# Mixer D's scores from stacked fp32r parts of queries and keys

## The chip, the core and the metric

The kernel runs on one core of a Trainium2 chip. The metric is the device time of one execution in microseconds: 2028.61 us is the median of three runs of the kernel before (2028.13 to 2029.02). A core has TensorE (PE in the profile, its weight loads PEld), VectorE (DVE), ScalarE (ACT), GpSimd (POOL, not used here) and SyncE (SP), which issues most of the DMAs.

## The reference

It is a two-layer encoder trunk: 512 positions, 1024 channels, float32. In each layer one projection feeds four mixers; their outputs are projected, gated, summed and projected again, and a squared-ReLU MLP follows. The change touches mixer D, a dilated sliding-window attention with three groups (window, dilation) of four heads of 64 channels:

```
D_PATTERNS = ((128, 1), (512, 4), (2048, 16))

def mixer_d(q, k, v, cs):                     # q, k, v: 3 groups x 4 heads x 64, rotary on q and k
    for gi, (window, dil) in enumerate(D_PATTERNS):
        # every dil-th position forms a sequence of its own
        o, lse = banded_attention(to_residue(q)..., to_residue(k), to_residue(v), window // (2 * dil), 64)
        ...
    wts = softmax(stack(lses))                # the groups are combined by their softmax denominators
    out = sum(wts[..., None] * stack(outs))

def banded_attention(q, k, v, half_window, block, sink=None):
    sc = einsum(q, k) * hd ** -0.5            # the scores
    sc = where(|kpos - qpos| <= half_window, sc, -1e30)
    p = exp(sc - max(sc)); l = sum(p)
    o = einsum(p, v) / l;  lse = max(sc) + log(l)
```

## The kernel before

**Numbers.** TensorE takes plain fp32 in more than one pass, and fp32r, a float32 with a shorter mantissa, in one. Nearly all large products are written as three fp32r products: every operand is split into a high part (a cast to fp32r) and a low part (what the cast dropped), and high x high, high x low and low x high are summed in PSUM (`mm3`, lines 177 to 179). Weights come as chunks of 128x1024 floats: SP loads a chunk (`raw`, L102), ACT casts it (`whi`, L118), DVE subtracts (`wlo`, L127). `ahead` keeps three chunks loaded and three split before the one in use.

Mixers A and C have their scores in fp32r already, in two products. Their stored queries hold the high part on 64 partitions and the low part on the other 64, stacked, and their keys hold the same high part on both halves, and then the same low part on both; one product of the stack with the doubled high keys and one with the doubled low keys give all four part products (L796, L797).

**Mixer D before.** Queries and keys lie in DRAM (`qD`, `kD`: group, head, 64 channels, 512 positions; in groups 1 and 2 the positions are sorted by residue). `attn_d` loads a group as one tile of queries and one of keys, `Qd` and `Kd`, two heads stacked on the partitions and two side by side, two groups ahead of the first step and the third at the first step of group 1. The heads are walked in 16 steps: in group 0 two steps a head, each with two blocks of 128 queries against 192 or 256 keys; in groups 1 and 2 one step a head, with four blocks of 128 by 128. The scores are plain fp32 products over 64 partitions:

```
nc.tensor.matmul(ps[:, r * 128:(r + 1) * 128], Q[:, r * 128:(r + 1) * 128], K[:, r * 128:(r + 1) * 128])
```

**A step's parts.** Scores (PE into one of two banks `ps_s`); `exps`: DVE adds the mask and takes the maximum (L941, L946 in group 0; L957, L959, L960 in groups 1 and 2), ACT takes the exponentials (L949, L962); `transposes` (PE into `ps_t`, L977, plain fp32); `copies` back to SBUF (L990 on ACT, L988 on DVE where a block has 64 rows); `values` (PE into `ps_o`, plain fp32, L1003 and L1009), with `og` copied out by ACT (L1016, L1018).

**What sets the order.** Every engine runs its instructions in the order in which the code records them. `pipeline` lets steps overlap: in iteration i stand the values of step i-5, the copies of step i-4, the transposes of step i-3, the scores of step i and the exponentials of step i-1:

```
yield from self.pipeline(steps, [("v", 5), ("c", 4), ("t", 3), ("s", 0), ("e", 1)])
```

`merge` lets this generator alternate with `fill`, which records the gate logits and output projection of another branch (here C): fp32r matmuls of 512 columns (L177 to L179), pieces of 6 or more between two iterations, and their results' work on DVE and ACT (L719, L720 gates; L726, L727 gated sums). `MG[2] = (18, 47, 12)` puts twelve of fill's pieces between the first yield of `attn_d`, at which its loads are issued, and its first step. On PE an iteration thus reads: values, transposes, scores, then a row of projection matmuls. Waits between engines are semaphores, set where one touches what another wrote; SP's loads are issued in order too.

Of the kernel before, what the change touches and what calls it, by code (L numbers as in the profile page):

```python
# [11 lines left out]
F32 = mybir.dt.float32  # L12
F32R = mybir.dt.float32r
I32 = mybir.dt.int32
AF = mybir.ActivationFunctionType
ALU = mybir.AluOpType
# [4 lines left out]
DM, S, DEPTH, HD = 1024, 512, 2, 64  # L21
# [54 lines left out]
class Body:  # L76
# [62 lines left out]
    def lows(self):  # L139
        while self.n_lo < self.n_split:  # L140
            self.wlo()
# [622 lines left out]
    def attn_gqa(self, l, which, y):  # L764
# [20 lines left out]
        def step(h, i):  # L785
# [13 lines left out]
            def exps():  # L799
                ps = st["s"]  # L800
                P = st["P"] = ap.tile([128, S], F32, tag="P", name="P", bufs=4)
                m, nm, ls = self.smt(1, "am"), self.smt(1, "an"), self.smt(1, "al")
# [21 lines left out]
            def norm():  # L824
                P, ls = st["P"], st["l"]
                if not isA:
# [62 lines left out]
    def attn_d(self, l, y):  # L889
        nc, ap = self.nc, self.ap  # L890
        nv, ns = nc.vector, nc.scalar
        QK, OG, PO = {}, {}, {}
# [3 lines left out]
        wd = self.drp.tile([12, S], F32, tag="wd", name="wd")  # L896
        steps = []

        def load(g):
            QK[g] = []  # L900
            for src, tag in ((self.qD, "Qd"), (self.kD, "Kd")):
                t = ap.tile([128, 2, S], F32, tag=tag, name=tag, bufs=2)
                nc.sync.dma_start(out=t, in_=src[g].rearrange("(a b) d t -> (b d) a t", b=2))
                QK[g].append(t)

        def window(c):
            return (64, 256) if c == 0 else (0, 192) if c == 3 else (0, 256)
# [1 line left out]
        def step(g, h, u, first, last):  # L909
            hp, o = h // 2, 64 * (h % 2)  # L910
            st = {}

            def scores():
                if first and 0 < g < 2:
                    load(g + 1)
                Q, K = (t[o:o + 64, hp] for t in QK[g])
                ps = st["s"] = self.ps("s")
                if g == 0:
                    for w in range(2):
                        c = 2 * u + w  # L920
                        lo, hi = window(c)
                        k0 = c * 128 - 64
                        nc.tensor.matmul(
                            ps[:, w * 256 + lo:w * 256 + hi], Q[:, c * 128:(c + 1) * 128], K[:, k0 + lo:k0 + hi]
                        )
                else:
                    for r in range(4):
                        nc.tensor.matmul(
                            ps[:, r * 128:(r + 1) * 128], Q[:, r * 128:(r + 1) * 128], K[:, r * 128:(r + 1) * 128]
                        )  # L930

            def exps():
                ps = st["s"]
                P = st["P"] = ap.tile([128, S], F32, tag="P", name="P", bufs=4)
                if g == 0:
                    for w in range(2):
                        c = 2 * u + w
                        lo, hi = window(c)
                        m = self.smt(1, "am")
                        Pw = P[:, w * 256 + lo:w * 256 + hi]  # L940
                        nv.tensor_tensor_reduce(  # L941
                            out=Pw, in0=ps[:, w * 256 + lo:w * 256 + hi], in1=self.cs[:, C_M1 + lo:C_M1 + hi],
                            scale=1.0, scalar=-3.0e38, op0=ALU.add, op1=ALU.max, accum_out=m,
                        )
                        nm = ML[0][:, c, 0, h:h + 1]
                        nv.tensor_scalar(  # L946
                            out=nm, in0=m, scalar1=self.nrs8[:, c:c + 1], scalar2=None, op0=ALU.mult
                        )
                        ns.activation(  # L949
                            out=Pw, in_=Pw, func=AF.Exp, scale=self.rs8[:, c:c + 1], bias=nm,  # L950
                            accum_out=ML[0][:, c, 1, h:h + 1],
                        )
                else:
                    mo = C_M2 if g == 1 else C_M3
                    P3, ps3 = (t.rearrange("p (r k) -> p r k", r=4) for t in (P, ps))
                    mk = self.cs[:, mo:mo + 128].rearrange("p (o k) -> p o k", o=1).to_broadcast([128, 4, 128])
                    nv.tensor_tensor(out=P3, in0=ps3, in1=mk, op=ALU.add)  # L957
                    m = self.smt(4, "dm")
                    nv.tensor_reduce(out=m, in_=P3, axis=AX.X, op=ALU.max, negate=True)  # L959
                    nv.tensor_tensor(out=ML[g][:, :, 0, h], in0=m, in1=self.rs8p, op=ALU.mult)  # L960
                    for r in range(4):
                        ns.activation(  # L962
                            out=P3[:, r], in_=P3[:, r], func=AF.Exp, scale=self.rs8p[:, r:r + 1],
                            bias=ML[g][:, r, 0, h:h + 1], accum_out=ML[g][:, r, 1, h:h + 1],
                        )

            def transposes():
                P = st.pop("P")
                pt = st["t"] = self.ps("t")
                st["n"] = []  # L970
                for b in range(4):
                    lo, n = 0, 128
                    if g == 0 and u == 0 and b == 0:
                        lo, n = 64, 64
                    if g == 0 and u == 1 and b == 3:
                        n = 64
                    nc.tensor.transpose(  # L977
                        pt[0:n, b * 128:(b + 1) * 128], P[:, b * 128 + lo:b * 128 + lo + n], self.ident
                    )
                    st["n"].append(n)  # L980

            def copies():
                pt = st["t"]
                PT = st["T"] = ap.tile([128, S], F32, tag="ptd", name="ptd", bufs=2)
                full = [b for b in range(4) if st["n"][b] == 128]
                for b in range(4):
                    if b not in full:
                        nv.tensor_copy(PT[0:64, b * 128:(b + 1) * 128], pt[0:64, b * 128:(b + 1) * 128])  # L988
                a, z = full[0] * 128, (full[-1] + 1) * 128
                ns.copy(PT[:, a:z], pt[:, a:z])  # L990

            def values():
                PT = st.pop("T")
                if h % 2 == 0 and u == 0:
                    PO[g, hp] = self.ps("o", 1)
                po = PO[g, hp]
                vcol = slice(h * 64, (h + 1) * 64)
                if g == 0:
                    for w in range(2):
                        c = 2 * u + w  # L1000
                        for z in range(2):
                            n = 64 if (c, z) in ((0, 0), (3, 1)) else 128
                            nc.tensor.matmul(  # L1003
                                po[o:o + 64, c * 128:(c + 1) * 128], self.VD[0:n, c + z, vcol],
                                PT[0:n, (2 * w + z) * 128:(2 * w + z + 1) * 128], start=(z == 0), stop=(z == 1),
                            )
                else:
                    for r in range(4):
                        nc.tensor.matmul(  # L1009
                            po[o:o + 64, r * 128:(r + 1) * 128], self.VD[:, (5, 9)[g - 1] + r, vcol],  # L1010
                            PT[:, r * 128:(r + 1) * 128],
                        )
                if h % 2 == 1 and (g > 0 or u == 1):
                    og = ap.tile([128, S], F32, tag=f"og{g}{hp}", name="og", bufs=1)
                    if g == 0:
                        ns.copy(og, po)  # L1016
                    else:
                        ns.copy(  # L1018
                            og.rearrange("p (a r) -> p r a", r=4), po.rearrange("p (r a) -> p r a", r=4)
                        )  # L1020
                    OG[g, hp] = og
                if last:
                    pat = "(c p) n -> p c n" if g == 0 else "(p c) n -> p c n"
                    nc.sync.dma_start(
                        out=mld[g].rearrange(pat, c=4), in_=ML[g].rearrange("p c m h -> p c (m h)")
                    )

            return dict(s=scores, e=exps, t=transposes, c=copies, v=values)

        load(0)  # L1030
        load(1)
        yield
        for g in range(3):
            units = [(h, u) for h in range(4) for u in range(2 if g == 0 else 1)]
            for n, (h, u) in enumerate(units):
                steps.append(step(g, h, u, n == 0, n == len(units) - 1))
# [450 lines left out]
```

## Time and profile before

| what | us |
|---|---|
| median of three runs | 2028.61 |
| the profiled execution | 2031.43 |
| its span (first to last instruction) | 2029.6 |
| PE busy in it | 2007.9 (99%) |
| PEld busy | 1662.9 (82%) |
| DVE busy | 1271.1 (63%) |
| ACT busy | 974.3 (48%) |

PE's busy time counts from a matmul's start to its modelled end, and consecutive matmuls overlap in it; how long one holds up the next is seen from the distance of their starts. A plain fp32 matmul leaves two records (128 records of L928 are 64 matmuls), an fp32r one leaves one, and the types of TensorE's operands read f32 in both cases. Mixer D runs in two places of the span: from 467 to about 563 us in the first layer and from 1470 to about 1566 us in the second.

### The profile page before, as it was taken

The page shows a single profiled execution, that of the slowest core. Times are in us where ns is not written, and L with a number is a line of the kernel's source. Part 1 is how long each engine was busy: PE and PEld are TensorE (multiplying, and loading weights), DVE is VectorE, ACT ScalarE, POOL GpSimd, SP SyncE. Part 2 cuts the span into 40 slices and gives each one's busy share as a digit, 9 for nine tenths or more (in the row PEclk, how much of TensorE's full clock was granted, in tenths as well). Part 3 has the DMA queues.
Part 4 walks back from the last instruction along what each step waited for, and adds up shares of the span by engine and source line. Part 5 has one row for each costly group of instructions (what it writes and reads, how often), then busy time and mean ns, then how long its engine had stood idle before and what let it go on. Part 6 is the DMA issues. An engine that isn't in the chain of part 4 may idle for free.

```text
span 2029.6 us, 25695 instructions
## 1 busy us (share of the span) xinstructions
PE 2007.9 (99%) x9752; PEld 1662.9 (82%) x9752; DVE 1271.1 (63%) x2274; ACT 974.3 (48%) x1701; POOL 0.2 (0%) x4
## 2 busy tenths in 40 slices
PE   9999999999999999999999999999999999999998
PEld 7888789887778888888878888898877888888887
DVE  6879775764466544544658897758644665444445
ACT  4357786854534332322323668868445344322322
POOL 0000000000000000000000000000000000000000
PEclk9999999999999999999999999999999999999999
DMA  5454424332134222323335552152421532323231
GB/s 190 145 156 135 130 66 147 117 125 83 51 106 146 95 95 94 103 94 104 119 109 166 156 166 94 59 163 91 135 73 46 173 96 93 103 94 94 93 104 63
DMA packets 87439, 227.03 MB, mean 112 GB/s; under 512 B 15098, under 2 KB 21370, under 8 KB 87316
## 3 DMA queue, kind: packets, MB, share of 16 engines
q1 hardware_dynamic: 84436, 221.20, 34.3%
q10 hardware_dynamic: 2880, 4.20, 0.6%
q8 instruction: 77, 1.26, 0.3%
q14 instruction: 46, 0.38, 0.1%
HBM read 201.08 MB, written 24.27 MB: 111 GB/s over the span
## 4 chain that ended last, share of the span: by engine, by line
PE 92%; DVE 3%; DMA 2%; ACT 2%; issue 1%; SPq 1%; DVEq 0%; ACTq 0%
PE ps_mm L177 14%; PE ps_mm L178 13%; PE ps_mm L179 13%; PE ps_t L177 6%; PE ps_t L179 6%; PE ps_t L178 6%; PE ps_s L177 6%; PE ps_s L179 6%; PE ps_s L178 6%; PE ps_o L856 2%; PE ps_t L835 2%; PE ps_s L796 1%; PE ps_s L797 1%; PE ps_o L1003 1%; PE ps_t L977 1%
## 5 line engine op out<-in xcount | busy, mean ns | idle before, releaser
L118 ACT CAST whi<-raw 128x1024 fp32r<-128x1024 f32 (+1 forms) x318 | 329.2, 1041 | 333.7 <-PE ps_mm L178 105.9
L127 DVE TENSOR_TENSOR wlo<-raw,whi 128x1024 fp32r<-128x1024 f32 (+1 forms) x318 | 384.8, 1214 | 96.8 <-ACT whi L118 93.9
L177 PE MATMUL ps_mm<-xh,whi 128*128 128x512 f32 x720 | 288.8, 401 | 0.0
L179 PE MATMUL ps_mm<-xh,wlo 128*128 128x512 f32 x720 | 282.4, 392 | 0.0
L178 PE MATMUL ps_mm<-xl,whi 128*128 128x512 f32 x720 | 282.3, 392 | 0.0
L177 PEld LDWEIGHTS ps_mm<-xh,whi 128*128 128x128 f32 x720 | 135.9, 189 | 32.4 <-issue 4.1
L179 PEld LDWEIGHTS ps_mm<-xh,wlo 128*128 128x128 f32 x720 | 135.9, 189 | 29.9
L178 PEld LDWEIGHTS ps_mm<-xl,whi 128*128 128x128 f32 x720 | 136.1, 189 | 26.8
L177 PE MATMUL ps_t<-xh,whi 128*128 128x512 f32 x368 | 143.6, 390 | 0.0
L179 PE MATMUL ps_t<-xh,wlo 128*128 128x512 f32 x368 | 143.3, 389 | 0.0
L178 PE MATMUL ps_t<-xl,whi 128*128 128x512 f32 x368 | 143.2, 389 | 0.0
L177 PE MATMUL ps_s<-xh,whi 128*128 128x512 f32 x352 | 138.5, 393 | 0.0
L179 PE MATMUL ps_s<-xh,wlo 128*128 128x512 f32 x352 | 137.0, 389 | 0.0
L178 PE MATMUL ps_s<-xl,whi 128*128 128x512 f32 x352 | 137.0, 389 | 0.0
L845 DVE TENSOR_TENSOR PT<-ps_t,PT 128x512 fp32r<-128x512 f32 (+2 forms) x128 | 75.1, 587 | 64.3 <-ACT PT L842 56.3
L829 ACT ACTIVATE P<-P,al 128x512 f32<-128x512 f32 (+2 forms) x128 | 82.6, 645 | 17.0 <-DVE al L828 15.7
L719 DVE TENSOR_TENSOR gt<-ps_mm,rb 128x512 f32<-128x512 f32 x54 | 37.2, 689 | 78.9 <-PE ps_mm L179 78.5
L842 ACT CAST PT<-ps_t 128x512 fp32r<-128x512 f32 (+2 forms) x128 | 63.8, 500 | 47.4 <-PE ps_o L856 43.9
L177 PEld LDWEIGHTS ps_t<-xh,whi 128*128 128x128 f32 x368 | 69.1, 188 | 17.2 <-issue 3.0
L179 PEld LDWEIGHTS ps_t<-xh,wlo 128*128 128x128 f32 x368 | 69.1, 188 | 14.9 <-DVE wlo L127 0.5
L178 PEld LDWEIGHTS ps_t<-xl,whi 128*128 128x128 f32 x368 | 69.1, 188 | 14.2
L177 PEld LDWEIGHTS ps_s<-xh,whi 128*128 128x128 f32 x352 | 66.1, 188 | 14.8 <-issue 1.4
(423 smaller groups left out, 4213.5 us busy)
## 6 DMA issues: line engine op xcount, KB each, us to landing
raw<-in_w_dram SPq DMA_DIRECT2D x314, 512.0 KB, 3.5
qsA<-stk SPq DMA_DIRECT2D x32, 128.0 KB, 2.3
qsC<-stk SPq DMA_DIRECT2D x32, 128.0 KB, 2.3
K<-ks SPq DMA_DIRECT2D x16, 256.0 KB, 6.3
Q<-qsA SPq DMA_DIRECT2D x16, 256.0 KB, 3.7
Q<-qsC SPq DMA_DIRECT2D x16, 256.0 KB, 5.1
qD<-stkf SPq DMA_DIRECT2D x24, 128.0 KB, 2.2
kD<-stkf SPq DMA_DIRECT2D x24, 128.0 KB, 2.3
```

The costliest lines, as they stand in the source:

```text
L118: self.nc.scalar.copy(hi[:, s], self.raws[i][:, s])
L127: self.nc.vector.tensor_tensor(out=lo[:, s], in0=raw[:, s], in1=hi[:, s].bitcast(F32), op=ALU.subtract)
L177: mm(ps, sh, mh, start=(k == 0), stop=False)
L178: mm(ps, sh, ml, start=False, stop=False)
L179: mm(ps, sl, mh, start=False, stop=(k == n - 1))
L719: nv.tensor_tensor(out=g, in0=ps, in1=self.rb, op=ALU.mult)
L796: nc.tensor.matmul(ps[:, 0:n], qq, Kt[j][:, 0, b0 * 128:b1 * 128], start=True, stop=False)
L829: ns.activation(out=P[:, 0:n], in_=P[:, 0:n], func=AF.Copy, scale=ls)
L835: nc.tensor.transpose(pt[:, b * 128:(b + 1) * 128], P[:, b * 128:(b + 1) * 128], self.ident)
L842: ns.copy(st["dst"][0], st["src"])
L845: nv.tensor_tensor(out=st["dst"][1], in0=st["src"], in1=st["dst"][0].bitcast(F32), op=ALU.subtract)
L856: nc.tensor.matmul(o, a, b, start=(n_ == 0), stop=(n_ == len(mm) - 1))
```

## The change

Queries and keys of mixer D are loaded by head instead of by group, twice each, onto both halves of the partitions (`Qr`, plain floats, two buffers; the second half of `Kd`, three buffers). `highs(n)` casts both on ACT: all 128 rows of the queries into `Qd`, and the keys into the first half of `Kd`. `lows(n)` subtracts on DVE: rows 64 to 127 of `Qd` become the queries' low part, and the second half of `Kd` the keys' low part. The scores then are two fp32r products of each block, over 128 partitions, as in mixers A and C. The load of head n+2 stands behind the scores of head n, its casts ahead of that head's exponentials, its subtractions behind that head's mask; the first two heads are loaded where the groups were, and cast and subtracted just ahead of the first step. Masks, exponentials, transposes, copies and values are as before.

```
+        def load(n):
+            g, h = heads[n]
+            q = ap.tile([128, S], F32, tag="Qr", name="Qr", bufs=2)
+            k = ap.tile([128, 2, S], F32R, tag="Kd", name="Kd", bufs=3)
+            for z in range(2):
+                nc.sync.dma_start(out=q[64 * z:64 * (z + 1)], in_=self.qD[g, h])
+                nc.sync.dma_start(out=k[64 * z:64 * (z + 1), 1].bitcast(F32), in_=self.kD[g, h])
+        def highs(n):
+            qs = ap.tile([128, S], F32R, tag="Qd", name="Qd", bufs=2)
+            ns.copy(qs, q)
+            ns.copy(k[:, 0], k[:, 1].bitcast(F32))
+        def lows(n):
+            nv.tensor_tensor(out=qs[64:128], in0=q[64:128], in1=qs[64:128].bitcast(F32), op=ALU.subtract)
+            nv.tensor_tensor(out=k[:, 1], in0=k[:, 1].bitcast(F32), in1=k[:, 0].bitcast(F32), op=ALU.subtract)
...
             def scores():
-                Q, K = (t[o:o + 64, hp] for t in QK[g])
+                n = 4 * g + h
+                Q, K = QK[n]
...
+                for o, q0, k0, w in blocks:
+                    for z in range(2):
                         nc.tensor.matmul(
-                            ps[:, w * 256 + lo:w * 256 + hi], Q[:, c * 128:(c + 1) * 128], K[:, k0 + lo:k0 + hi]
+                            ps[:, o:o + w], Q[:, q0:q0 + 128], K[:, z, k0:k0 + w], start=(z == 0), stop=(z == 1)
                         )
+                if g > 0 or u == 1:
+                    QK.pop(n)
+                    if n + 2 < len(heads):
+                        load(n + 2)
...
             def exps():
+                n = 4 * g + h + 2
+                ahead = (g > 0 or u == 1) and n < len(heads)
+                if ahead:
+                    highs(n)
...
+                if ahead:
+                    lows(n)
...
         load(0)
         load(1)
         yield
+        for n in range(2):
+            highs(n)
+            lows(n)
```

On PE, at the first step of group 1 in the first layer, before (L1003 are values, L977 transposes, L928 scores, L177 the next projection matmul; xN counts equal neighbours):

```order
L1003 MATMUL ps_o<-ptd,VD 64x128 x4
L977 MATMUL ps_t<-cs,P 128x128 x3
L977 MATMUL ps_t<-cs,P 64x128
L928 MATMUL ps_s<-Kd,Qd 128x128 x4
L177 MATMUL ps_mm<-xh,whi 128x512
```

And with the change (the same lines have the numbers 1031, 1005 and 946 now):

```order
L1031 MATMUL ps_o<-ptd,VD 64x128 x4
L1005 MATMUL ps_t<-cs,P 128x128 x3
L1005 MATMUL ps_t<-cs,P 64x128
L946 MATMUL ps_s<-Kd,Qd 128x128 x8
L177 MATMUL ps_mm<-xh,whi 128x512
```

The scores stay between the transposes and the projection matmuls; four plain matmuls have become eight fp32r ones.

On DVE, ahead of the first mask of the first layer, before (L726 and L727 are the gated sums of two chunks, L941 the mask, L946 the scaled maximum):

```order
L127 TENSOR_TENSOR wlo<-raw,whi 128x1024
L726 SCALAR_TENSOR_TENSOR gt<-gt,ps_mm 128x512
L727 TENSOR_TENSOR mg<-mg,gt 128x512
L726 SCALAR_TENSOR_TENSOR gt<-gt,ps_mm 128x512
L727 TENSOR_TENSOR mg<-mg,gt 128x512
L941 ISA P,am<-ps_s,cs 128x192
```

With the change (L921 and L922 are `lows`, L967 is the mask):

```order
L127 TENSOR_TENSOR wlo<-raw,whi 128x1024
L726 SCALAR_TENSOR_TENSOR gt<-gt,ps_mm 128x512
L727 TENSOR_TENSOR mg<-mg,gt 128x512
L921 TENSOR_TENSOR Qd<-Qr,Qd 64x512
L922 TENSOR_TENSOR Kd<-Kd 128x512
L921 TENSOR_TENSOR Qd<-Qr,Qd 64x512
L922 TENSOR_TENSOR Kd<-Kd 128x512
L726 SCALAR_TENSOR_TENSOR gt<-gt,ps_mm 128x512
L727 TENSOR_TENSOR mg<-mg,gt 128x512
L967 ISA P,am<-ps_s,cs 128x192
```

The subtractions of the first two heads stand between the gated sums of two chunks, ahead of the first mask, and the first scores wait for the first pair of them.

On ACT, at the first steps of group 1 in the first layer, before (L990 copies transposes, L962 are exponentials, L118 and L720 work for the projections):

```order
L118 CAST whi<-raw 128x1024
L720 ACTIVATE gt<-gt,d_hb 128x512
L990 COPY ptd<-ps_t 128x384
L962 ACTIVATE P,ML_4733<-P,ML_4733,rs8p 128x128 x4
L990 COPY ptd<-ps_t 128x384
L962 ACTIVATE P,ML_4733<-P,ML_4733,rs8p 128x128 x4
```

With the change (L915 and L916 are `highs`, L1018 the copies, L988 the exponentials):

```order
L118 CAST whi<-raw 128x1024
L720 ACTIVATE gt<-gt,d_hb 128x512
L1018 COPY ptd<-ps_t 128x384
L915 CAST Qd<-Qr 128x512
L916 CAST Kd<-Kd 128x512
L988 ACTIVATE P,ML_4733<-P,ML_4733,rs8p 128x128 x4
L1018 COPY ptd<-ps_t 128x384
L915 CAST Qd<-Qr 128x512
L916 CAST Kd<-Kd 128x512
L988 ACTIVATE P,ML_4733<-P,ML_4733,rs8p 128x128 x4
```

Two casts have come ahead of the exponentials of each step that prepares a later head. On SP the loads change in the same way: before, four loads of 512 KB stand ahead of the first step and two at the start of group 1; now eight of 128 KB stand ahead, and four more for each later head, one or two heads between two weight loads.

## Rows read from the trace of the kernel before

**Rows 1.** The page: span, engines' busy time, the chain's shares by engine

```profile
span 2029.6 us, 25695 instructions
...
PE 2007.9 (99%) x9752; PEld 1662.9 (82%) x9752; DVE 1271.1 (63%) x2274; ACT 974.3 (48%) x1701; POOL 0.2 (0%) x4
...
PE 92%; DVE 3%; DMA 2%; ACT 2%; issue 1%; SPq 1%; DVEq 0%; ACTq 0%
```

**Rows 2.** Stretches, layer 1: length; PE, PEld, DVE, ACT, POOL busy; clock; DMA

```profile
467.20:505.00 37.80, 37.80 (x180) 27.23 (x179) 19.78 (x65) 16.11 (x40) 0.00 (x0) 1.00 0.22 76
505.00:551.00 46.00, 46.00 (x260) 35.45 (x259) 21.94 (x38) 26.91 (x79) 0.00 (x0) 1.00 0.16 45
```

**Rows 3.** PE's timeline at the first scores: start, length, engine, line, operation, tiles, form

```profile
460.14 0.39 PE L179 MATMUL ps_mm<-xh,wlo 128*128 128x512 f32 x1
...
466.94 0.39 PE L179 MATMUL ps_mm<-yC,wlo 128*128 128x512 f32 x1
467.25 1.02 PE L923 MATMUL ps_s<-Kd,Qd 64*128 64x192 f32 x4
468.21 0.50 PE L177 MATMUL ps_mm<-xh,whi 128*128 128x512 f32 x1
468.54 0.40 PE L178 MATMUL ps_mm<-xl,whi 128*128 128x512 f32 x1
```

**Rows 4.** PE's timeline: transposes, scores, projection; groups 0 and 2

```profile
498.73 0.63 PE L977 MATMUL ps_t<-cs,P 128*64 128x128 f32 x4
499.29 1.02 PE L923 MATMUL ps_s<-Kd,Qd 64*128 64x256 f32 x4
...
500.58 0.40 PE L178 MATMUL ps_mm<-xl,whi 128*128 128x512 f32 x1
...
544.41 0.66 PE L977 MATMUL ps_t<-cs,P 128*128 128x128 f32 x4
544.99 1.16 PE L928 MATMUL ps_s<-Kd,Qd 64*128 64x128 f32 x8
...
546.42 0.40 PE L178 MATMUL ps_mm<-xl,whi 128*128 128x512 f32 x1
```

**Rows 5.** PE's timeline: transposes and projection without scores between

```profile
550.04 0.66 PE L977 MATMUL ps_t<-cs,P 128*128 128x128 f32 x4
...
550.77 0.39 PE L178 MATMUL ps_mm<-xl,whi 128*128 128x512 f32 x1
```

**Rows 6.** Weight loads of scores: a block's; all of L928, shortest, median, longest

```profile
510.70 0.96 PEld L928 LDWEIGHTS ps_s<-Kd,Qd 64*128 64x128 f32 x8 [0.17 <-issue]
...
L928 PEld LDWEIGHTS ps_s<-Kd,Qd x128: 182/188/188, 505.0 to 1548.9; 64*128 64x128 f32 x128
```

**Rows 7.** PE's timeline in mixer C: fp32r scores, transposes, fp32r matmuls

```profile
362.59 0.28 PE L796 MATMUL ps_s<-K,Q 128*128 128x256 f32 x1
362.71 0.28 PE L797 MATMUL ps_s<-K,Q 128*128 128x256 f32 x1
362.82 0.49 PE L835 MATMUL ps_t<-cs,P 128*128 128x128 f32 x3
363.07 0.36 PE L177 MATMUL ps_mm<-whi,xh 128*128 128x256 f32 x1
363.27 0.28 PE L178 MATMUL ps_mm<-wlo,xh 128*128 128x256 f32 x1
```

**Rows 8.** ACT and DVE ahead of the first scores; casts and subtractions of 128x512

```profile
462.70 0.72 ACT L720 ACTIVATE gt<-gt,d_hb 128x512 f32<-128x512 f32 x1
...
465.37 0.69 DVE L727 TENSOR_TENSOR mg<-mg,gt 128x512 f32<-128x512 f32 x1
...
L870 ACT CAST yC<-yt 128x512 fp32r<-128x512 f32 x8 | 5.0, 621 | 0.7 <-DVE yt L868 0.4
...
L874 DVE TENSOR_TENSOR yC<-yt,yC 128x512 fp32r<-128x512 f32 x8 | 5.5, 686 | 1.4 <-ACT yC L870 1.4
```

**Rows 9.** DMA issues: tiles, queue, count, KB each, median us to landing

```profile
qD<-stkf SPq DMA_DIRECT2D x24, 128.0 KB, 2.2
...
Kd<-kD SPq DMA_DIRECT2D x6, 512.0 KB, 6.0
```

More of the change, by code (lines that the diff above doesn't have):

```diff
@@ L897, in attn_d @@
         steps = []
[L899 to L904, printed above, removed]
+        heads = [(g, h) for g in range(3) for h in range(4)]
+        def load(n):
[5 more added lines that the diff above has]
+                nc.sync.dma_start(out=k[64 * z:64 * (z + 1), 1].bitcast(F32), in_=self.kD[g, h])
+            QK[n] = [q, k]
+        def highs(n):
+            q, k = QK[n]
+            qs = ap.tile([128, S], F32R, tag="Qd", name="Qd", bufs=2)
+            ns.copy(qs, q)
+            ns.copy(k[:, 0], k[:, 1].bitcast(F32))
+            QK[n] = [qs, k, q]
+        def lows(n):
+            qs, k, q = QK[n]
+            nv.tensor_tensor(out=qs[64:128], in0=q[64:128], in1=qs[64:128].bitcast(F32), op=ALU.subtract)
+            nv.tensor_tensor(out=k[:, 1], in0=k[:, 1].bitcast(F32), in1=k[:, 0].bitcast(F32), op=ALU.subtract)
+            QK[n] = [qs, k]
         def window(c):
@@ L913, in scores @@
             def scores():
-                if first and 0 < g < 2:
-                    load(g + 1)
-                Q, K = (t[o:o + 64, hp] for t in QK[g])
+                n = 4 * g + h
+                Q, K = QK[n]
                 ps = st["s"] = self.ps("s")
                 if g == 0:
+                    blocks = []
                     for w in range(2):
@@ L921, in scores @@
                         lo, hi = window(c)
-                        k0 = c * 128 - 64
+                        blocks.append((w * 256 + lo, c * 128, c * 128 - 64 + lo, hi - lo))
+                else:
+                    blocks = [(r * 128, r * 128, r * 128, 128) for r in range(4)]
+                for o, q0, k0, w in blocks:
+                    for z in range(2):
                         nc.tensor.matmul(
-                            ps[:, w * 256 + lo:w * 256 + hi], Q[:, c * 128:(c + 1) * 128], K[:, k0 + lo:k0 + hi]
+                            ps[:, o:o + w], Q[:, q0:q0 + 128], K[:, z, k0:k0 + w], start=(z == 0), stop=(z == 1)
                         )
[L926 to L930, printed above, removed]
+                if g > 0 or u == 1:
+                    QK.pop(n)
+                    if n + 2 < len(heads):
+                        load(n + 2)
             def exps():
```

## The prediction

> **What bounds the kernel now.** I read the page first: its totals and its chain of waits. TensorE is busy 99% of the 2029.6 us and the chain that ended last runs through it for 92% [rows 1]. So a change is worth what it takes from, or adds to, the row of matmuls on PE, unless it starves that row. Second came the busy times of the only stretch that the change touches, mixer D in the first layer: in its 83.8 us PE has no free time at the full granted clock of 1.00, while DVE is busy 41.7 us and ACT 43.0 [rows 2]. The second layer repeats it a thousand microseconds later. Third came PE's timeline there. A busy PE is not a PE at its peak, so I read starts, not durations: from L179 at 460.14 to L179 at 466.94 there are 30 fp32r matmuls of 512 columns, (466.94 - 460.14) / 30 = 0.227 us each, back to back [rows 3]. Whatever lies between two such groups costs the distance of the starts around it, less the matmuls that belong to the groups.
>
> **What one block of scores costs today.** Each layer has 16 steps: eight in group 0 (two blocks of 192 and 256 columns each) and eight in groups 1 and 2 (four blocks of 128). A plain fp32 matmul leaves two records, so a step leaves 4 or 8.
> Group 0 straight after projection matmuls: from L179 at 466.94 to the second L178 behind it at 468.54 is 1.60 us. Two pitches of 0.227 in it belong to the groups: 1.60 - 0.45 = 1.15 us [rows 3]. This is so for the first three steps of a layer, where no transposes stand ahead yet.
> Group 0 behind transposes: from the first L977 at 498.73 to L178 at 500.58 is 1.85 us [rows 4]. Where a step has no scores any more, the same distance is 550.77 - 550.04 = 0.73 us [rows 5]. The block costs 1.12 us (five steps a layer).
> Groups 1 and 2: 546.42 - 544.41 - 0.73 = 1.28 us (eight steps a layer) [rows 4, 5].
> A part of that is no arithmetic. The weight loads of one such block are eight within 0.96 us of 0.188 each, so (0.96 - 0.188) / 7 = 0.110 us apart, and the matmuls follow at about 0.112: eight of them are 0.90 us [rows 6]. The other 0.38 us lie at the two edges of the block, where the next weights are not loaded ahead.
>
> **What it costs after.** The stacked parts need two fp32r matmuls for each block, over 128 rows. The count of records stays the same, 4 and 8; what changes is the price of one and the edges.
> Edges: mixer C has just this sequence already, fp32r scores (L796, L797), then transposes, then fp32r matmuls of 256 columns. L796 to L797 is 0.12 us, L797 to the first of three transposes 0.11, and from that transpose to the second fp32r matmul behind 363.27 - 362.82 = 0.45, which is three transposes of 0.11 and one matmul of 0.12 [rows 7]. No edge is left on either side, and I take none for the new blocks.
> Price: 256 columns at 0.12 us [rows 7]. For 192 and 128 columns in fp32r the trace has no row. From below: the line through 0.12 at 256 columns and 0.227 at 512 gives 0.093 and 0.066. From above: four passes as plain fp32, two records of 0.112 at 128 columns, so 0.224, and 0.336 at 192. I take 0.112 for both: a weight load of 128 columns stands ahead of each, the same number of columns as in the loads that are 0.110 apart now, and that row is the nearest [rows 6].
> Group 0 becomes 2 x 0.112 + 2 x 0.12 = 0.46 us, groups 1 and 2 become 8 x 0.112 = 0.90 us.
> Saved over both layers: 6 x (1.15 - 0.46) + 10 x (1.12 - 0.46) + 16 x (1.28 - 0.90) = 4.1 + 6.6 + 6.1 = 16.8 us. All of it lies on PE's row.
>
> **The added work.** Each of 24 heads gets two casts on ACT, each 128x512 to fp32r, 0.62 us by the nearest row, and two subtractions on DVE, 0.69 each (the 64-row one taken as dear) [rows 8]. Heads 2 to 11 of each layer do this a step or more early. ACT's cover: in the 46 us of groups 1 and 2 it is busy 26.9; six pairs of casts add 7.4, in a stretch that shrinks to 42.9 us, so 34.3 of 42.9, 80%. DVE there goes from 21.9 to 30.2. In the 37.8 us of group 0 it goes from 19.8 to about 28 of 32.9, ACT from 16.1 to 21.1 [rows 2]. Neither reaches its limit. A cast delays the exponentials behind it, but the order has the transposes that read them two steps later, over 4 us each, and weights are split three chunks ahead. I take nothing for these; without the cover, each head could cost up to 1.24 us.
> The first head has no such cover. Its casts stand behind L720, which ends at 462.70 + 0.72 = 463.42, and are done by 464.7. Its subtractions stand on DVE behind L727, which ends at 465.37 + 0.69 = 466.06, and end at 466.06 + 2 x 0.69 = 467.44 [rows 8]. PE is ready at 466.94 + 0.227 = 467.17 [rows 3]. With about 0.1 for the hand-over PE waits 0.4 us, once a layer: +0.8 us. Head 1's subtractions then hold up the gated products (L726) and the first mask by some 1.4 us, which the two score banks and the same two steps cover.
> SP issues four loads of 128 KB a head instead of two of 512 KB a group. A store of 128 KB lands in 2.2 us, the present loads of 512 KB in up to 6.0 [rows 9]. In the order they are free to go once the scores of the head before are done and the weight load ahead of them on SP has gone, at least a step ahead of their cast. I take nothing.
> Sum: -16.8 + 0.8 = -16.0 us. The profiled execution took 2031.43 us, 2.8 above the median, so it would be 2015.4, and the median 2028.61 - 16.0 = 2012.6.
>
> **Rivals.**
> *Narrow fp32r matmuls pay plain fp32's price* (0.224 and 0.336 us). Then group 0 costs 0.67 + 0.24 = 0.91 and groups 1 and 2 1.79: the first saves 6 x 0.24 + 10 x 0.21 = 3.5, the second loses 16 x 0.51 = 8.2, and with the 0.8 it is +5.5: 2034.1, slower. For it: no fp32r row here is under 256 columns. Against it: the rows at 256 and 512 lie near one line, and nothing in them bends up. There are 128 matmuls of 128 columns and 32 of 192; the change turns into a loss once their mean price passes 0.112 + 16.0 / 160 = 0.21 us.
> *The price falls under the weight load's spacing*, to 0.066 and 0.093: 128 x 0.046 + 32 x 0.019 = 6.5 more: 2006.1. Against it: no loads of 128 columns there come closer than about 0.11. The Trainium skill (TensorE: Matmul & The Clock Gate, "Back-to-back issue gap") puts a stream of load and matmul pairs of 128 columns at about 81 ns each; by that, as an estimate, 160 x 0.031 = 5.0 us more would be saved, 2007.6. The loads 0.110 apart speak against it, but they are plain fp32 and so don't settle it.
> *The edges stay*: 32 x 0.38 = 12.2 us of the saving is not there: 2024.8. For it: the step keeps plain fp32 products and transposes ahead of the scores. Against it: mixer C's rows.
> *The split heads come late.* ACT and DVE take their work in order, so a cast that waits for its load holds up exponentials, and a subtraction that waits for its cast holds up the split of a weight. With half a microsecond of it reaching PE for each of the 20 covered heads, that is +10: 2022.6. For it: SP puts loads behind weight loads that wait for DVE, so the three queues close a ring. Against it: the idle shares above. The same skill page ("Architectural detail: the array is 16x 32x32, not 1x 128x128") calls ACT's and DVE's queues strictly first in, first out; the rows fit that and show no price.
>
> **Chances.** Forecast 0.69 (its own range 2010 to 2016, for the wait and a pitch from 0.107 to 0.12), late heads 0.11, edges 0.07, fp32's price 0.07, cheaper than the load 0.06. From 2007 to 2024 lie the first two and about half of the last, the others outside. What can be told from no change is 0.2%, 4.1 us. Faster by more than that: 0.69 + 0.06 + 0.09 of the late heads + 0.02 of the edges = 0.86; within: the rest of the edges, 0.02 of late heads and 0.01 of fp32's price, 0.08; slower 0.06.
>
> **What would show it.** Right: a score record of 128 columns every 0.11 us and of 256 every 0.12, the first L178 after a block of groups 1 and 2 at 0.73 + 0.90 us from the first transpose, a stretch of mixer D about 8 us shorter in each layer, one PE wait of some 0.4 us ahead of a layer's first scores, for DVE. Wrong: a spacing near 0.22, edges of 0.2 us left, or PE waiting inside the stretch for Qd, Kd, wlo or the copies of ACT.

## The result, and the profile after

The changed kernel takes 2013.55 us in the median of four runs (2011.35 to 2016.16) against 2028.37 of the kernel before on the same chip (2027.1 to 2029.02): a ratio of 0.9927, 95% interval 0.9915 to 0.9939, 14.8 us less. Forecast were 2012.6 us and 16.0 less. The profiled execution took 2011.35 us.

The page after answers to [rows 1]; the columns are an engine's busy time, its share and its instructions, then the chain's shares:

```profile
span 2009.6 us, 26003 instructions
...
PE 1988.3 (99%) x9752; PEld 1657.4 (82%) x9752; DVE 1300.8 (65%) x2322; ACT 998.2 (50%) x1749; POOL 0.2 (0%) x4
...
PE 93%; DVE 3%; ACT 2%; DMA 1%; issue 1%; SPq 0%; DVEq 0%; ACTq 0%
```

PE still bounds the kernel. Its count of records is the same, 9752, and its busy time fell by 19.6 us; DVE gained 29.7 us of work and ACT 23.9, which the chain does not show.

Next the whole span cut at mixer D, with the columns of [rows 2]. Of before:

```profile
0.00:467.20 467.20, 460.76 (x2372) 388.95 (x2372) 350.00 (x730) 293.09 (x532) 0.20 (x4) 1.00 0.42 134
467.20:562.50 95.30, 95.30 (x506) 71.69 (x506) 46.55 (x111) 49.74 (x133) 0.00 (x0) 1.00 0.20 62
562.50:1470.30 907.80, 902.53 (x4318) 754.04 (x4317) 581.37 (x996) 432.78 (x709) 0.00 (x0) 1.00 0.37 117
1470.30:1565.60 95.30, 95.30 (x506) 71.67 (x506) 46.55 (x111) 49.75 (x133) 0.00 (x0) 1.00 0.20 62
```

And the same stretches of after:

```profile
0.00:464.10 464.10, 458.66 (x2372) 387.83 (x2373) 350.79 (x732) 295.60 (x535) 0.20 (x4) 1.00 0.42 132
464.10:551.00 86.90, 86.76 (x506) 69.44 (x506) 60.63 (x134) 59.50 (x153) 0.00 (x0) 1.00 0.42 117
551.00:1459.50 908.50, 902.77 (x4318) 754.32 (x4318) 582.11 (x998) 434.60 (x712) 0.00 (x0) 1.00 0.37 116
1459.50:1546.40 86.90, 86.76 (x506) 69.44 (x505) 60.74 (x134) 59.54 (x153) 0.00 (x0) 1.00 0.43 117
```

The two stretches of mixer D went from 95.3 to 86.9 us, 16.8 together. The rest of this pair of profiles differs by 3.1 us ahead of the first mixer D and by less than a microsecond in each part behind it, where nothing was changed. A part of the 3.1 is one stretch in which before shows 0.50 of the granted clock (1.2 GHz in place of 2.4) after PE waited 2.2 us for a load of mixer A's queries, and after does not. Before, then after:

```profile
210.67:214.08 3.41, 3.41 (x10) 2.63 (x9) 3.38 (x9) 3.39 (x7) 0.00 (x0) 0.50 1.04 275
```

```profile
210.67:214.08 3.41, 3.41 (x16) 2.83 (x16) 3.38 (x6) 3.38 (x4) 0.00 (x0) 1.00 0.67 225
```

So the profiled pair differs by 20.1 us and the medians by 14.8; the length of the stage is the better measure. I take it from PE's starts, from the record ahead of a layer's first score to the first record behind its last values (505 steps from record to record): 95.29 us before and 86.84 to 86.86 after, 8.44 to 8.45 less a layer. A second set of runs of the changed kernel gave 86.85 and 86.86, although its profiled execution took 2018.01 us in all. Below, "the stage" is this length.

Now PE's timeline of after at the places of [rows 3] and [rows 4]: the first scores, a block of group 0 and one of group 2 behind transposes (the latter with the values ahead of them):

```profile
463.93 0.39 PE L179 MATMUL ps_mm<-yC,wlo 128*128 128x512 f32 x1
464.16 1.00 PE L946 MATMUL ps_s<-Kd,Qd 128*128 128x192 f32 x4
465.00 0.40 PE L177 MATMUL ps_mm<-xh,whi 128*128 128x512 f32 x1
465.23 0.39 PE L178 MATMUL ps_mm<-xl,whi 128*128 128x512 f32 x1
...
491.22 0.63 PE L1005 MATMUL ps_t<-cs,P 128*64 128x128 f32 x4
491.60 0.68 PE L946 MATMUL ps_s<-Kd,Qd 128*128 128x256 f32 x4
492.12 0.41 PE L177 MATMUL ps_mm<-xh,whi 128*128 128x512 f32 x1
492.38 0.39 PE L178 MATMUL ps_mm<-xl,whi 128*128 128x512 f32 x1
...
532.28 1.09 PE L1037 MATMUL ps_o<-ptd,VD 128*64 128x128 f32 x8
533.30 0.66 PE L1005 MATMUL ps_t<-cs,P 128*128 128x128 f32 x4
533.71 1.09 PE L946 MATMUL ps_s<-Kd,Qd 128*128 128x128 f32 x8
534.64 0.45 PE L177 MATMUL ps_mm<-xh,whi 128*128 128x512 f32 x1
534.93 0.40 PE L178 MATMUL ps_mm<-xl,whi 128*128 128x512 f32 x1
```

By the prediction's own measure the block of group 2 now costs 534.93 - 533.30 - 0.73 = 0.90 us (0.90 forecast), that of group 0 behind transposes 492.38 - 491.22 - 0.73 = 0.43 (0.46). The rows and columns of the array that a matmul uses, called its tile below, stand behind the operands' names: `64*128` for the scores in [rows 3, 4], `128*128` here. Keep an eye on them.

The first block of a layer takes 465.23 - 463.93 - 0.45 = 0.85; the next one, 917 ns between the same two records, costs 0.46. So 0.39 us are a wait, and the groups of PE's weight loads by releaser name it (busy, mean ns | idle before, its releaser):

```profile
L946 PEld LDWEIGHTS ps_s<-Kd,Qd 128*128 128x128 f32 x192 | 24.5, 191 | 1.2 <-DVE Kd L922 0.9
```

DVE's timeline there, as forecast, has the subtractions behind L727:

```profile
462.36 0.69 DVE L727 TENSOR_TENSOR mg<-mg,gt 128x512 f32<-128x512 f32 x1
463.08 0.69 DVE L921 TENSOR_TENSOR Qd<-Qr,Qd 64x512 fp32r<-64x512 f32 x1
463.80 0.69 DVE L922 TENSOR_TENSOR Kd<-Kd 128x512 fp32r<-128x512 f32 x1
```

The keys' low part is done at 464.49. PE was ready at 463.93 + 0.23 = 464.16 and started the block's first product then; the second, which reads the low part, followed 0.39 us later. No other block of scores waits: the 0.9 us are two times, one a layer. The loads that feed the heads take longer than the store of 128 KB that I had read (count, KB each, median us from issue to landing; [rows 9]), with no wait of PE from it:

```profile
Qr<-qD SPq DMA_DIRECT2D x48, 128.0 KB, 3.9
Kd<-kD SPq DMA_DIRECT2D x48, 128.0 KB, 4.0
```

ACT did wait for them: six of the 24 casts of queries stood 9.9 us in all for their load. The longest of these waits:

```profile
477.87 0.62 ACT L915 CAST Qd<-Qr 128x512 fp32r<-128x512 f32 x1 [2.84 <-DMA Qr<-qD]
```

### The profile page after: what moved, and what is told of

It is laid out like the page before. It is cut to its first block, busy times and chain, and to the rows that moved or that the text cites. A ratio compares the mean times of both kernels' runs of the same rounds, so it can differ in the third digit from the quotient of the medians.

```text
span 2009.6 us, 26003 instructions
## 1 busy us (share of the span) xinstructions
PE 1988.3 (99%) x9752; PEld 1657.4 (82%) x9752; DVE 1300.8 (65%) x2322; ACT 998.2 (50%) x1749; POOL 0.2 (0%) x4
## 4 chain that ended last, share of the span: by engine, by line
PE 93%; DVE 3%; ACT 2%; DMA 1%; issue 1%; SPq 0%; DVEq 0%; ACTq 0%
PE ps_mm L177 14%; PE ps_mm L178 14%; PE ps_mm L179 14%; PE ps_t L177 6%; PE ps_t L179 6%; PE ps_t L178 6%; PE ps_s L177 6%; PE ps_s L178 6%; PE ps_s L179 6%; PE ps_o L856 2%; PE ps_t L835 2%; PE ps_s L796 1%; PE ps_s L797 1%; PE ps_s L946 1%; PE ps_o L1031 1%; PE ps_t L1005 1%
## 5 line engine op out<-in xcount | busy, mean ns | idle before, releaser
L118 ACT CAST whi<-raw 128x1024 fp32r<-128x1024 f32 (+1 forms) x318 | 329.1, 1041 | 302.6 <-PE ps_mm L178 94.1
L177 PE MATMUL ps_mm<-xh,whi 128*128 128x512 f32 x720 | 286.3, 398 | 0.0
L179 PE MATMUL ps_mm<-xh,wlo 128*128 128x512 f32 x720 | 281.7, 391 | 0.0
L179 PEld LDWEIGHTS ps_mm<-xh,wlo 128*128 128x128 f32 x720 | 135.6, 188 | 29.7
L177 PEld LDWEIGHTS ps_mm<-xh,whi 128*128 128x128 f32 x720 | 135.7, 188 | 27.3 <-issue 0.8
L177 PE MATMUL ps_t<-xh,whi 128*128 128x512 f32 x368 | 143.6, 390 | 0.0
L179 PE MATMUL ps_t<-xh,wlo 128*128 128x512 f32 x368 | 143.3, 389 | 0.3 <-DVE wlo L127 0.3
L177 PE MATMUL ps_s<-xh,whi 128*128 128x512 f32 x352 | 138.5, 394 | 0.0
L179 PE MATMUL ps_s<-xh,wlo 128*128 128x512 f32 x352 | 137.0, 389 | 0.0
L829 ACT ACTIVATE P<-P,al 128x512 f32<-128x512 f32 (+2 forms) x128 | 82.6, 645 | 16.9 <-DVE al L828 15.7
L177 PEld LDWEIGHTS ps_t<-xh,whi 128*128 128x128 f32 x368 | 69.1, 188 | 17.2 <-issue 3.0
L179 PEld LDWEIGHTS ps_t<-xh,wlo 128*128 128x128 f32 x368 | 69.1, 188 | 15.1 <-DVE wlo L127 0.7
L177 PEld LDWEIGHTS ps_s<-xh,whi 128*128 128x128 f32 x352 | 66.1, 188 | 14.8 <-issue 1.4
L178 PEld LDWEIGHTS ps_s<-xl,whi 128*128 128x128 f32 x352 | 66.1, 188 | 14.0 <-issue 0.5
```

What stands on the lines that cost most here:

```text
L118: self.nc.scalar.copy(hi[:, s], self.raws[i][:, s])
L177: mm(ps, sh, mh, start=(k == 0), stop=False)
L178: mm(ps, sh, ml, start=False, stop=False)
L179: mm(ps, sl, mh, start=False, stop=(k == n - 1))
L829: ns.activation(out=P[:, 0:n], in_=P[:, 0:n], func=AF.Copy, scale=ls)
```

## The experiments

My theory: a block of scores lost its two edges, 0.38 us, because fp32r matmuls have none where plain fp32 has them, and kept the price of 0.112 us a record; the added work is covered. Rivals: that part of the saving comes from elsewhere in the change (other loads, other order), and that the edges belong to something else than the number format.

**Groups 1 and 2 alone.** Group 0 keeps plain fp32 scores over 64 rows, and its heads are loaded but neither cast nor subtracted. The edit of the scores:

```
+                    if g == 0:
+                        nc.tensor.matmul(ps[:, o:o + w], Q[0:64, q0:q0 + 128], K[0:64, 1, k0:k0 + w].bitcast(F32))
+                        continue
```

> Heads of group 0 are loaded as with the change but neither cast nor subtracted, and their scores are plain fp32 matmuls over 64 rows again; groups 1 and 2 are as changed. Theory (each block of scores is worth its own difference on PE's row): the blocks of groups 1 and 2 cost 0.90 us and the 16 of group 0 1.12 to 1.15 again, so 16 x 0.38 = 6.1 us under the kernel before, about 2022.3; no wait ahead of the first scores. Rival (a good part of the gain lies outside the score blocks, in a shorter chain at the end of mixer D or ahead of it): the time lies well under that, near 2016, or near the kernel before.

Measured: 2024.1 us, ratio 0.9976 (0.9965 to 0.9987). The stage is 92.08 us, 3.21 less than before in each layer: eight blocks at 0.38 are 3.1. Group 0 is back at the distances of before (1606, 1490 ns), groups 1 and 2 stand at 1240. The time is 1.8 above the expected one, within what whole runs vary; the stage says that groups 1 and 2 bring about what the sum gave them.

**The feeding alone.** All loads, casts and subtractions, but the scores as before, from the plain copies, which have three buffers here:

```
+            kx = ap.tile([128, 2, S], F32R, tag="Kd", name="Kd", bufs=1)
+            ns.copy(kx[:, 0], k)
...
+            nv.tensor_tensor(out=kx[:, 1], in0=k, in1=kx[:, 0].bitcast(F32), op=ALU.subtract)
...
+                    nc.tensor.matmul(ps[:, o:o + w], Q[0:64, q0:q0 + 128], K[0:64, k0:k0 + w])
```

> All of the added work (four loads a head, two casts, two subtractions at the same places) is there, but its results go unused: the scores are plain fp32 matmuls from the loaded tiles. Theory (the added work is covered): the time of the kernel before, 2028.4, within 1 us; ACT is some 30 us and DVE some 32 us busier over both layers, and PE does not wait for them. Rival (late heads): half a microsecond or more for each of 20 heads reaches PE, 2038 or more.

Measured: 2028.79 us, ratio 0.9998 (0.9989 to 1.0008). The stage is 95.29 us in both layers, as before. The added work costs nothing where PE doesn't wait for its result, and the rival of the late heads falls.

**Half the moving columns.** In groups 1 and 2 the second product has 64 keys in place of 128:

```
+                        v = w // 2 if g > 0 and z == 1 else w
...
-                            ps[:, o:o + w], Q[:, q0:q0 + 128], K[:, z, k0:k0 + w], start=(z == 0), stop=(z == 1)
+                            ps[:, o:o + v], Q[:, q0:q0 + 128], K[:, z, k0:k0 + v], start=(z == 0), stop=(z == 1)
```

> In groups 1 and 2 the second product of each block (with the keys' low part) takes only the first 64 of its 128 columns; the low part of the other keys is left out. Theory (the weight load of 128 columns sets the spacing of narrow fp32r matmuls): the starts in a block stay about 0.11 us apart and the block stays at 0.90 us. Rival (the moving columns set it): the four short ones take about half, and the block falls to about 0.70 us, 3 us in all.

Measured: 2012.24 us in one run, the stage 86.97. PE's timeline:

```profile
534.32 0.66 PE L1006 MATMUL ps_t<-cs,P 128*128 128x128 f32 x4
534.73 1.06 PE L947 MATMUL ps_s<-Kd,Qd 128*128 128x128 f32 x8
535.62 0.47 PE L177 MATMUL ps_mm<-xh,whi 128*128 128x512 f32 x1
535.93 0.40 PE L178 MATMUL ps_mm<-xl,whi 128*128 128x512 f32 x1
```

535.93 - 534.32 = 1.61 against 1.63: at 128 and 64 columns the moving operand is not what sets the price of an fp32r record.

**Half the stationary columns.** The second product of groups 1 and 2 takes only 64 of the 128 queries, and the sums of both products are left out:

```
+                        m = 64 if g > 0 and z == 1 else 128
...
-                            ps[:, o:o + w], Q[:, q0:q0 + 128], K[:, z, k0:k0 + w], start=(z == 0), stop=(z == 1)
+                            ps[0:m, o:o + w], Q[:, q0:q0 + m], K[:, z, k0:k0 + w], start=(g > 0 or z == 0), stop=(g > 0 or z == 1)
```

> As the changed kernel, but in groups 1 and 2 the second of the two products of a block has only 64 queries as its stationary operand and overwrites half of the rows (the sums are left out). Halving the moving columns left the spacing at 0.11 us. Theory that the load of the stationary columns sets it: records after a 64-column load stand some 0.055 us closer, four to a block, so a block's stretch goes from 1.24 to about 1.02 us, and 16 of them give 3.5 us: 2010 us. Rival, that each matmul has a fixed price whatever its operands: 1.24 us and 2013.5 us. Second rival, that the change between 64 and 128 columns costs what the change of rows costs, some 0.1 us at each turn: 1.6 us and 2019 us.

Measured: 2010.38 us in one run, the stage 85.33 to 85.35, 1.5 less a layer.

```profile
535.02 0.66 PE L1006 MATMUL ps_t<-cs,P 128*128 128x128 f32 x4
535.44 0.88 PE L947 MATMUL ps_s<-Kd,Qd 128*128 128x128 f32 x8
536.15 0.44 PE L177 MATMUL ps_mm<-xh,whi 128*128 128x512 f32 x1
536.43 0.39 PE L178 MATMUL ps_mm<-xl,whi 128*128 128x512 f32 x1
```

536.43 - 535.02 = 1.41 in place of 1.63; the spacings of records alternate between about 62 and 112 ns where all were 109 to 115. So the price of 0.11 us of an fp32r record goes with its 128 stationary columns. The Trainium skill (TensorE: Matmul & The Clock Gate, "LDWEIGHTS (loading the stationary operand)") says that a weight load takes time by its columns and not by its rows, by its formula 107 ns for 128 and 53 for 64; the spacings of 0.11 and 0.06 agree. The expectation's second rival fell too. In this run half of the records use 64 columns of the array, in turn with those that use 128:

```profile
L947 PE MATMUL ps_s<-Kd,Qd 128*64 128x128 f32 x64 | 11.8, 224 | 0.0
```

None of these turns shows an edge.

**The stacked operands as plain fp32.** The same tiles over 128 rows, read as plain fp32:

```
-                            ps[:, o:o + w], Q[:, q0:q0 + 128], K[:, z, k0:k0 + w], start=(z == 0), stop=(z == 1)
+                            ps[:, o:o + w], Q[:, q0:q0 + 128].bitcast(F32), K[:, z, k0:k0 + w].bitcast(F32), start=(z == 0), stop=(z == 1)
```

> The same stacked tiles over 128 rows, but the score products are plain fp32 matmuls, two records each. Theory (the edges of 0.2 us belong to plain fp32 matmuls): they are there on both sides of a block; groups 1 and 2 cost 16 x 0.112 + 0.38 = 2.17 us a block, group 0 4 x 0.162 + 4 x 0.216 + 0.38 = 1.89, so 43 us over the changed kernel, about 2056. Rival (the edges came from operands of 64 rows): no edges, 1.79 and 1.51 us, about 2044.

Measured: 2043.39 us in one run, the stage 102.3.

```profile
533.25 0.65 PE L1005 MATMUL ps_t<-cs,P 128*128 128x128 f32 x4
533.75 1.95 PE L946 MATMUL ps_s<-Kd,Qd 128*128 128x128 f32 x16
535.45 0.48 PE L177 MATMUL ps_mm<-yC,whi 128*128 128x512 f32 x1
535.77 0.39 PE L178 MATMUL ps_mm<-yC,whi 128*128 128x512 f32 x1
```

The block costs 535.77 - 533.25 - 0.73 = 1.79 us for 16 records, 0.112 each: plain fp32, and no edge. My theory's cause falls here. What is different from before is the tile, `128*128` in place of `64*128`.

**fp32r over 64 rows.** The changed kernel, with the products cut to the first 64 rows, so that the products with the queries' low part are left out:

```
-                            ps[:, o:o + w], Q[:, q0:q0 + 128], K[:, z, k0:k0 + w], start=(z == 0), stop=(z == 1)
+                            ps[:, o:o + w], Q[0:64, q0:q0 + 128], K[0:64, z, k0:k0 + w], start=(z == 0), stop=(z == 1)
```

> As the changed kernel, but the scores' matmuls of mixer D read only the first 64 rows of the stacked tiles (the products with the queries' low parts are left out); same count, same 128x128x... blocks, fp32r. From the end of the matmul records before a block to the second projection matmul behind it the changed kernel shows 1238 to 1246 ns in groups 1 and 2 and 802 to 810 ns in group 0 behind transposes, without a gap at either edge. Theory that a gap comes with a change between operands of 64 and of 128 rows: about 1.4 to 1.65 us and 1.0 to 1.2 us, with 0.15 to 0.2 us at one edge or both, and some 2019 us in all. Rival, that the gap needs a plain fp32 matmul of 64 rows: 1.24 and 0.81 us as now, and 2013.5 us.

Measured: 2022.56 us in one run, the stage 92.59.

```profile
534.68 0.66 PE L1005 MATMUL ps_t<-cs,P 128*128 128x128 f32 x4
535.27 1.11 PE L946 MATMUL ps_s<-Kd,Qd 64*128 64x128 f32 x8
536.30 0.50 PE L177 MATMUL ps_mm<-xh,whi 128*128 128x512 f32 x1
536.64 0.40 PE L178 MATMUL ps_mm<-xl,whi 128*128 128x512 f32 x1
```

536.64 - 534.68 - 0.73 = 1.23: the edges are back with fp32r. Record by record, against the changed kernel: from the last transpose to the first score 203 ns in place of 29, from the last score to L177 200 in place of 110, and 68 more in the pitches next to these. With the run before, all four cases are there: plain and fp32r, over 64 rows with edges, over 128 without. The cause is the change between 64 and 128 rows from the scores to their neighbours. What happens at an edge shows in PE's weight loads, here and in the changed kernel:

```profile
535.27 0.96 PEld L946 LDWEIGHTS ps_s<-Kd,Qd 64*128 64x128 f32 x8 [0.17 <-issue]
```

```profile
533.69 0.97 PEld L946 LDWEIGHTS ps_s<-Kd,Qd 128*128 128x128 f32 x8
```

Over 64 rows the block's first load starts together with its matmul, 0.17 us after the loads of the transposes; over 128 rows it follows them at once. The Trainium skill (TensorEngine Tiling (Array Packing), "Key Properties") says that a change of the tiling mode drains TensorE; these rows fit that for the rows of the array and give a price, 0.33 us in fp32r and 0.38 in plain fp32 for going to 64 rows and back.

**Values in pairs.** The values (plain fp32 products of 64 stationary columns, tile `128*64`) pay such edges too: 318 ns from L179 to their first record in place of 227, and 203 to the next transposes in place of 109. What brings these edges is not shown: the 64 columns alone don't, since the half-weight scores above have none, and neither have the transposes, which go from `128*128` to `128*64` in 109 ns. So the products of two steps were recorded together:

```
+                second = (u if g == 0 else h) % 2
+                held.append((g, h, u, PT))
+                if not second:
+                    return
+                for a in held:
+                    product(*a)
+                held.clear()
+                close()
```

(`product` and `close` are the two halves of `values` as it was. `ptd` has three buffers in place of two and `P` three in place of four, and a later tile that used `P`'s buffers takes one of `ptd`'s.) The changed kernel ran beside it:

> The changed kernel again, on the chip of the two that follow: 2013.5 us, 0.993 of the kernel before. Blocks of scores as before: 1.24 us in groups 1 and 2, 0.80 to 0.94 us in group 0, the first of a layer 1.30 us.

> The changed kernel with the products by the values of two steps emitted together, so that 16 of the 32 calls of values in the program have no other matmuls around them. Theory: each call pays some 0.14 us at its front edge and 0.15 us behind it, as the trace shows for values between projections and transposes; 16 calls fewer on an edge give 16 x 0.29 = 4.6 us, so 2009 us. Rival: the time at those edges is the wait of TensorE for the copies of the transposes and stays, or the later release of two tiles delays the next step as much as it saves: 2013.5 us or up to 2 us above it.

Measured: the changed kernel 2013.59 us, ratio 0.9929 (0.9915 to 0.9942); paired 2006.38, ratio 0.9892 (0.9876 to 0.9909). The stage went from 86.85 to 84.03, 5.6 us in both layers. The edges explain less than I had written: only 14 calls went, since the last two of a layer stood together before, and 14 x 0.29 is 4.1. More came from another side. It shows in PE's timeline of the paired kernel, group 2, against a single call, L1037 at 532.28 in the rows of after:

```profile
536.35 1.58 PE L1048 MATMUL ps_o<-ptd,VD 128*64 128x128 f32 x16
537.87 0.66 PE L1005 MATMUL ps_t<-cs,P 128*128 128x128 f32 x4
```

Sixteen records last 1.58 us, not 1.09 + 8 x 0.11 = 1.97. In the middle of the pair, where the second head's blocks follow the first one's, most starts are 52 to 58 ns apart. In group 0, where a pair is two halves of the same head, with the same output rows, they stay 109 apart. Six pairs are new, so 6 x 0.39 is 2.3, and with the 4.1 it would be 6.4; the pitches of the projection matmuls, 0.5 us longer in all, take back most of the difference to 5.6. What lengthened them is not shown.

**The first heads earlier.** The same, with the split of a layer's first two heads called ahead of the last pieces of the fill:

```
+MID = 7
...
+        yield
...
-        for _ in range(first):
+        for n in range(first):
             step(1)
+            if n == mid:
+                step(0)
```

> The kernel with paired values and, in addition, the split of the first two heads of a layer called four pieces of the fill earlier. Theory: the wait of 0.39 us before a layer's first scores goes, so 0.8 us below the kernel with paired values, 2008 us. Rival: the casts then stand in front of mixer C's last copies on ScalarE and VectorE, and the wait appears there instead: the same time as paired values alone, or up to 1 us above it.

Measured: 2005.84 us, ratio 0.989 (0.9874 to 0.9906); the stage 83.67, 0.37 less a layer. The first scores:

```profile
466.21 0.39 PE L180 MATMUL ps_mm<-yC,wlo 128*128 128x512 f32 x1
466.43 0.63 PE L947 MATMUL ps_s<-Kd,Qd 128*128 128x192 f32 x4
...
467.14 0.40 PE L179 MATMUL ps_mm<-xl,whi 128*128 128x512 f32 x1
```

467.14 - 466.21 = 0.93 in place of 1.30: the wait is gone. The medians of the two, half a microsecond apart, can't tell it; the stage can.

**Values alternated.** In addition, the two heads' products alternate block by block in groups 1 and 2:

```
+                    for r in range(4):
+                        for a in held:
+                            product(*a, r)
```

> The kernel with paired values and early split, with the products by the values of two heads of groups 1 and 2 alternated (a block of one head, then the same block of the other). In the trace of the paired kernel the records of two heads stand 52 to 58 ns apart in the middle of a pair, where blocks of both are at hand, and 109 ns apart at its ends. Theory: matmuls of 64 columns whose outputs lie in different halves of the rows run beside each other, so alternated blocks run so from first to last: the 14 spacings between the first and the last two records of a pair go from 1.14 to about 0.80 us, 0.3 to 0.4 us for each of 8 pairs, 2.4 to 3.2 us in all, 2003 us. Rival: what overlaps is only the turn from one head to the next; alternated blocks pay the change of columns at every matmul, as they do at the edges (0.05 to 0.1 us each), and a pair takes 0.3 us more: 2008 us.

Measured: 2003.85 us, ratio 0.9881 (0.9862 to 0.9901); the stage 81.89, 1.77 less a layer than without the alternation.

```profile
536.29 1.09 PE L1053 MATMUL ps_o<-ptd,VD 128*64 128x128 f32 x16
537.32 0.66 PE L1006 MATMUL ps_t<-cs,P 128*128 128x128 f32 x4
```

Sixteen records in 1.09 us, the time of eight in the changed kernel: the two heads, whose outputs lie on rows 0 to 63 and 64 to 127, run beside each other (starts 6 and 103 ns apart in turn). Three of four pairs take 0.49 us less and the last 0.31. This version beats both kernels: mixer D's stage is 4.96 us a layer shorter than in the changed kernel and 13.4 shorter than before.

## Why the prediction was right, and where its reason was not

*PE's row bounds mixer D, and a change is worth what it takes from that row.* Right: 16.8 us of the windows, and nothing elsewhere that the change touched.

*Blocks.* Forecast 0.46 and 0.90 us; measured 0.43 and 0.90. The forecast saving without the wait was 16.8 us. Measured from record to record it is 8.45 a layer and the 0.39 of the wait on top, 17.7 in both, 0.9 more than forecast: 0.6 of it lies in the pitches of the projection matmuls behind a block, from the second pitch on, where the forecast's distances end. By kinds of spacing, the 8.45 of the first layer are 5.98 at the edges of 16 blocks (into the scores, out of them, and the pitches behind) and 2.86 between the records within the blocks (2.30 in group 0, 0.56 in groups 1 and 2), less the 0.39.

*The edges vanish.* The size was right: 5.98 / 16 = 0.37 us a block, against 0.38. The words "the next weights are not loaded ahead" describe an edge rightly, as the weight loads above show. The step that failed is what I took to remove it, fp32r, with mixer C's fp32r rows as the pattern. Plain fp32 over 128 rows has no edge and fp32r over 64 rows has it. The change altered the format and the rows together, so the number held by luck. Mixer C's rows [rows 7] carried the right answer for another reason: its tiles are `128*128` like their neighbours', while `64*128` stands in every score row of [rows 3, 4, 6]. I read the one difference and not the other.

*The price of a record, 0.112 us at 128 columns.* Right for fp32r, and with the reason given, the weight load: half the moving columns left it, half the stationary columns took 0.05 off. But the row that I read it from has the same price for another reason. Plain fp32 records go by their moving columns: 0.112 us for 128, 0.162 for 192 and 0.216 for 256 in the kernel before, and 0.109 for 128 with 64 stationary columns, in the values. That both formats cost 0.11 at 128 by 128 is a coincidence, and so the number was partly luck here too. The rivals on either side fell. fp32's price came out for plain fp32 alone, by its doubled records. For the lower one the Trainium skill's 81 ns (TensorE: Matmul & The Clock Gate, "Back-to-back issue gap") would have needed closer records: the measured 0.109 to 0.115 decides against it here.

For groups 1 and 2 this means that fp32r as such gave next to nothing: eight records of 0.11 before, eight after. Of the 0.38 saved, 0.33 came from the use of 128 rows; the other 0.05, which fp32r over 64 rows had already, lie between the block's first two records. In group 0 the records are wider, and there a plain one costs more: 1.51 us for the eight of a block in the run with stacked plain operands is 0.19 each, against 0.46 / 4 = 0.12 in fp32r. Of the 0.69 saved there some 0.3 is the format and the rest the edges.

*The wait ahead of the first scores.* Forecast 0.4 us a layer for DVE's subtractions behind L727; measured 0.39, behind the block's first product and not ahead of it, and 0.37 came back once the split was earlier.

*The feeding costs nothing.* Right: the stage is the same to 0.01 us with all of it added. The reason held in part. I had taken the store's 2.2 us for a load of 128 KB, and it took 3.9 to 4.0, and I had the loads go at least a step ahead of their cast: six casts of queries waited for theirs all the same, by up to 2.8 us. PE's row shows no wait from it: heads did come late, and none reached PE.

*The sum.* 16.9 us measured in the stage against 16.0, and 14.8 in the medians, whose own spread is 2 to 5 us.

## What to carry to other kernels

Read the rows and columns (`64*128`, `128*64`, `128*128`) of every matmul in a row that bounds the time. Going to 64 rows and back cost 0.33 to 0.38 us a block here, and a call of the values with 64 columns some 0.29, so fill the rows, or put matmuls of one tile together. Not every turn costs: fp32r scores that changed from 128 to 64 columns and back had no edge, so test it on your own rows. Matmuls of half the columns whose outputs lie on different halves of the partitions are worth alternating. And where whole runs differ by microseconds, measure the stage from start to start.

## What the hardware showed that I had not expected

- Going from 128 to 64 rows and back cost 0.38 us in plain fp32 and 0.33 in fp32r. None of it shows as idle time of PE, which counts as busy; PE's weight loads show 0.17 us ahead of a block's first, put down to "issue".
- An fp32r record with 128 stationary columns cost 0.11 us for 128 moving columns and for 64, and 0.06 with 64 stationary columns. A plain fp32 record cost 0.11 for 128 moving columns with 128 stationary columns and with 64 alike, and plain fp32 has two records a matmul.
- Two streams of 64 stationary columns on different output rows ran at twice the rate when alternated (16 records in 1.09 us), and partly so when one merely followed the other (1.58), but not when both went to the same rows.
- The stage's length repeats within 0.02 us between executions whose whole times differ by up to 7 us.
